# Both scan directions of a bidirectional RWKV-7 mixer in one scheduled list, with bonus sums computed as rows

## The chip, the cores and the metric

The kernel runs on one core of one Trainium2 chip. The metric is the device time of one launch in microseconds (us), measured on the chip; lower is better.

## The reference

One layer of a hybrid backbone is applied to 4096 latent tokens and to 256 context tokens. Each token row of 1024 is normalised, modulated and projected. The projection feeds two branches: (A) a bidirectional RWKV-7 scan with 8 heads of 64, and (B) a chunked gating unit. Both are gated, concatenated and mapped by one output projection; a norm, a gate and the residual follow. Everything is float32. What matters here is the scan of branch A, once forward and once backward over the tokens, with separate parameters per direction:

```python
def step(s, inp):
    r_t, k_t, v_t, w_t, kk_t, b_t = inp
    sa = jnp.einsum('bhvk,bhk->bhv', s, -kk_t)
    s = (s * w_t[:, :, None, :] + sa[..., None] * b_t[:, :, None, :]
         + v_t[..., None] * k_t[:, :, None, :])
    return s, jnp.einsum('bhvk,bhk->bhv', s, r_t)
...
for d in range(2):
    ...
    y_d, s_d = _delta_scan(r, k_d, v, decay, kk, kk * a, s0[d], reverse=(d == 1))
    y = y + y_d
    bonus = bonus + jnp.sum(r * k_d * p['r_k'][d].astype(f32), axis=-1, keepdims=True) * v
```

The latent tokens start from given states, the context tokens from zero; the context's final states are outputs too.

## The kernel before

The program has four stages. phase1a and phase1b norm and project all tokens and leave their results in DRAM: h as a high and a low part (d_h), r and k (d_rk), normalised keys (d_kk), v, the gates and the mixed values of branch B. phase2 is the forward scan, phase3 the backward scan with the output projection. A float32 product of weights is made as three matmuls of high and low parts in the type float32r, so each weight is loaded, cast on ScalarE (ACT) and subtracted on VectorE (DVE) once (split_w, L243 to L245).

A scan handles 34 chunks of 128 tokens, 32 of the latent sequence and 2 of the context, and each chunk holds two halves of 64 tokens. For one chunk the parts are, in the order of the data:

- load_ops: lw, lk, lkn, lr load the inputs (L657 and L661) by DMA; all DMAs of the scans are issued on SyncE's queue (SP).
- prep_ops: tanh and up (L692) give decay and rate; cum (L711) is the running sum of log decay on DVE, once per chunk; z, zr, kg, xa, xk make the scaled keys Z and X; qk and qr make q on GpSimd (POOL). ab0 and ab1 (L769) multiply X with Z into PSUM, and four mask multiplies abm00, abm01, abm11, abm10 (L777) bring them to the tile AB on DVE.
- bon (L794) multiplies q with the block of bonus weights rkb, and bonc (L798) copies the 8 sums per token to the tile bo.
- diag (L786) writes the 16x16 diagonal blocks of AB to DRAM in eight small DMAs, blocks (L821) reads them back, spread over partitions, into Ab. step0 to step14 (L851 and L855, two DVE instructions each) invert them; keepT (L859) and place0, place1 (L864, eight DMAs) put the inverses in place in Qb; flip (L880) transposes them on DVE, and mm0 to mm3 (L873) with wm (L884) and ym0 to ym2 (L893) extend them to 64x64.
- scan_ops: for each half, zs (L933) and av (L941) on TensorE (PE), xsc (L951) on ACT, tu (L957) on PE, uv (L965) on ACT, sm (L970) and ys (L977) on PE, and su (L984, L985) on DVE, which updates the state S. zs of the next half reads S.

The forward scan also carries the projections of branch B (proj: L1042 on PE, h loaded at L1031 in two halves of 1 MB each for every 256 tokens). The backward scan adds the two directions (L1167), normalises (stats, scale, norm), gates, and runs the output projection (part0 to part11, L1260), squares, fin (L1286), finx and keepx. Its single-buffered tiles are zs, mb, the high and low parts of the mixed row (mh, ml), x and the result rows.

The order of the work is written by hand. Tables AT_FWD, AT_PROJ and AT_BWD give each part a time in units; pipeline() adds PERIOD = 30 units for each chunk, sorts all parts of one direction by these times and issues them in that order, so the tables set the order of instructions on each engine and of DMAs on SP. The waits are put in by the framework, from the regions that instructions read and write, and from buffers that come free. Each direction has a list of its own:

```python
evs += [(self.PERIOD * n + at[k], f) for k, f in parts.items()]
with self.tc.manual_schedule():
    for _, f in sorted(evs, key=lambda e: e[0]):
        f()
```

Between the two lists phase2's pools are closed, phase3 opens pools of the same kind, scan_setup builds masks and constants for direction 1, load_gp builds the output gain, gn_w and gn_b are loaded, and eight units of w_out are loaded and split through one staging buffer.

Of the kernel before, what the change touches and what calls it, by code (L numbers as in the profile page):

```python
# [2 lines left out]

# [4 lines left out]
F32 = mybir.dt.float32  # L8
# [17 lines left out]
class Mixer:  # L26
# [10 lines left out]
    def constants(self):  # L37
# [4 lines left out]
        self.stat = self.pool(self.ctx, "stat", bufs=4)  # L42
# [458 lines left out]
    def scan_setup(self, ctx, d):  # L501
        nc, io = self.nc, self.io
        self.d = d
        st = self.pool(ctx, f"st{d}")
        self.kp = self.pool(ctx, f"kp{d}", bufs=1)
        self.s1 = self.pool(ctx, f"s1{d}", bufs=1)
        self.s2 = self.pool(ctx, f"s2{d}", bufs=2)
        self.px = self.pool(ctx, f"px{d}", bufs=1, space=PSUM)
        self.dq = self.pool(ctx, f"dq{d}", bufs=3, space=DRAM)
        self.wup = st.tile([128, 512], F32, name="wup")  # L510
        for i, w in enumerate(("w_up", "a_up")):
            nc.sync.dma_start(self.wup[64 * i : 64 * i + 64], io[w][0, d])

        self.mask = st.tile([128, 2, 2, 64], F32, name="mask")
        sg = 1 if d == 0 else -1
        for X in range(2):
            for sl in range(2):
                for half in range(2):
                    nc.gpsimd.affine_select(
                        self.mask[64 * half : 64 * half + 64, X, sl, :], self.ones[64 * half : 64 * half + 64, 0:64],  # L520
                        pattern=[[sg, 64]], compare_op=ALU.is_ge, fill=0.0,
                        base=-1 if sl == X else 0, channel_multiplier=-sg,
                    )

        self.moff = st.tile([128, 4, 16], F32, name="moff")
        for half in range(2):
            nc.gpsimd.affine_select(
                self.moff[64 * half : 64 * half + 64],
                self.ones[64 * half : 64 * half + 64, 0:1].unsqueeze(2).to_broadcast([64, 4, 16]),
                pattern=[[-16 * sg, 4], [0, 16]], compare_op=ALU.is_ge, fill=0.0,  # L530
                base=-16 if d == 0 else -1, channel_multiplier=sg,
            )
        z = self.zero = 0 if d == 0 else 64
        self.run0 = st.tile([128, 8, 65], F32, name="run0")
        nc.vector.memset(self.run0, 1.0)
        nc.vector.memset(self.run0[:, :, z : z + 1], 0.0)
        self.inc = st.tile([128, 8, 65], F32, name="inc")
        nc.vector.memset(self.inc, 0.0)
        self.lnh = st.tile([128, 1], F32, name="lnh")
        nc.vector.memset(self.lnh, math.log(0.5))  # L540
        self.ka2 = st.tile([128, 4], F32, name="ka2")
        ka = self.ka = self.vT[:, 64 + 4 * d : 68 + 4 * d]
        nc.vector.tensor_scalar(self.ka2, ka, -1.0, 2.0, op0=ALU.mult, op1=ALU.add)
        self.rkb = st.tile([128, 4, 2], F32, name="rkb")
        nc.vector.memset(self.rkb, 0.0)
        rk = self.vT[:, 72 + 4 * d : 76 + 4 * d]
        for hh in range(2):
            sl = slice(64 * hh, 64 * hh + 64)
            nc.vector.tensor_scalar_mul(self.rkb[sl, :, hh], rk[sl], 0.25)
# [14 lines left out]

    @staticmethod
# [11 lines left out]
    def load_state(self, src):  # L577
        nc = self.nc
        if src is None:
            nc.gpsimd.memset(self.S, 0.0)  # L580
            return
        t = self.s1.tile([64, 4, 128], F32, name="stin", tag="q")
        nc.sync.dma_start(t.rearrange("v p (h k) -> v p h k", h=2), src.rearrange("(p h) v k -> v p h k", h=2))
        ps = self.px.tile([128, 256], F32, name="us", tag="us")
        for p in range(4):
            nc.tensor.transpose(ps[:, 64 * p : 64 * p + 64], t[:, p, :], self.ident[:64, :64])
        nc.vector.tensor_copy(self.S.rearrange("p a b -> p (a b)"), ps)

    def store_state(self, dst):
# [765 lines left out]
```

## Time and profile before

| | |
|---|---|
| time, median of 3 runs | 3635.41 us (3626.2 to 3649.29) |
| profiled execution | 3635.12 us, span 3633.4 us |
| TensorE clock granted, mean | 0.947 |
| PE, DVE, ACT, POOL busy | 89%, 57%, 34%, 28% |
| DMA | 429.61 MB, mean 118 GB/s |
| first and last cum forward | 1351.1 and 2383.5 us |
| first and last cum backward | 2477.9 and 3523.2 us |

In the profile L12 is line 12 of the kernel file. A group of instructions is named by line, engine, operation and out<-in, then the count, the busy time in us and the mean in ns of one, then the time for which its engine was idle just before them, with what ended it. PEld is the loading of weights on PE, which overlaps the matmuls. A float32 matmul shows as two instructions. SPq is the DMA queue of SyncE; a DMA's row there is its issue, not its transfer.

### The profile page before, as it was taken

The page shows a single profiled execution, that of the slowest core. Times are in us where ns is not written, and L with a number is a line of the kernel's source. Part 1 is how long each engine was busy: PE and PEld are TensorE (multiplying, and loading weights), DVE is VectorE, ACT ScalarE, POOL GpSimd, SP SyncE. Part 2 cuts the span into 40 slices and gives each one's busy share as a digit, 9 for nine tenths or more (in the row PEclk, how much of TensorE's full clock was granted, in tenths as well). Part 3 has the DMA queues.
Part 4 walks back from the last instruction along what each step waited for, and adds up shares of the span by engine and source line. Part 5 has one row for each costly group of instructions (what it writes and reads, how often), then busy time and mean ns, then how long its engine had stood idle before and what let it go on. Part 6 is the DMA issues. An engine that isn't in the chain of part 4 may idle for free. (4 is left out here: it accounts for less than half of the span.)

```text
span 3633.4 us, 102021 instructions
## 1 busy us (share of the span) xinstructions
PE 3238.2 (89%) x43093; PEld 2692.5 (74%) x43093; DVE 2059.3 (57%) x4969; ACT 1219.5 (34%) x2928; POOL 1005.1 (28%) x1500
## 2 busy tenths in 40 slices
PE   6999998799999968899898889873889899999997
PEld 4777776577887767888888888873777777777776
DVE  4455554322222235666666666654778787787884
ACT  3232231111111123343333333322444444444442
POOL 4444442111111111111111111110344444444443
PEclk9999999899999988999999999985899999999998
DMA  7354344522322133434343433424334444444442
GB/s 261 139 194 154 144 184 168 160 99 93 128 87 99 64 117 95 110 103 118 91 119 99 111 109 104 110 55 104 85 108 120 116 116 119 117 112 113 119 116 69
DMA packets 526870, 429.61 MB, mean 118 GB/s; under 512 B 191051, under 2 KB 458187, under 8 KB 519244
## 3 DMA queue, kind: packets, MB, share of 16 engines
q1 hardware_dynamic: 521386, 413.38, 37.1%
q10 hardware_dynamic: 5026, 9.70, 0.8%
q8 instruction: 339, 5.55, 0.7%
q14 instruction: 119, 0.97, 0.1%
HBM read 275.46 MB, written 147.46 MB: 116 GB/s over the span
## 5 line engine op out<-in xcount | busy, mean ns | idle before, releaser
L1042 PE MATMUL acc<-hld,wAh 128*128 128x256 f32 x2176 | 434.7, 300 | 13.3 <-DMA hld<-d_h 13.3
L1042 PEld LDWEIGHTS acc<-hld,wAh 128*128 128x128 f32 x2176 | 356.6, 201 | 25.1 <-DMA hld<-d_h 16.2
L1042 PE MATMUL acc<-hld,wAl 128*128 128x256 f32 x1088 | 317.6, 292 | 0.0
L851 DVE TENSOR_TENSOR tm<-TP,Ab 128x48 f32<-128x48 f32 (+13 forms) x1020 | 218.1, 214 | 156.1 <-DMA Ab<-dA 126.6
L777 DVE TENSOR_TENSOR AB<-prep,mask 128x512 f32<-128x512 f32 x272 | 177.1, 683 | 125.1 <-PE prep L769 122.0
L855 DVE TENSOR_TENSOR TP<-TP,tm 128x48 f32<-128x48 f32 (+13 forms) x1020 | 225.4, 221 | 35.1
L1260 PE MATMUL acc<-wAh,mh 128*128 128x512 f32 x544 | 242.1, 445 | 3.0 <-DVE on L1286 2.9
L272 PE MATMUL acc<-hl,wAh 128*128 128x512 f32 (+1 forms) x576 | 226.0, 395 | 0.0
L724 POOL TENSOR_TENSOR q<-q,k 128x512 f32<-128x512 f32 x68 | 97.3, 1431 | 457.5 <-ACT q L719 348.2
L1260 PE MATMUL acc<-wAl,mh 128*128 128x512 f32 x544 | 220.2, 405 | 0.0
L1260 PE MATMUL acc<-wAh,ml 128*128 128x512 f32 x544 | 220.1, 405 | 0.0
L272 PE MATMUL acc<-hh,wAl 128*128 128x512 f32 (+1 forms) x576 | 218.6, 384 | 0.0
L1042 PEld LDWEIGHTS acc<-hld,wAl 128*128 128x128 f32 x1088 | 217.8, 200 | 0.0
L272 PE MATMUL acc<-hh,wAh 128*128 128x512 f32 (+1 forms) x576 | 217.7, 393 | 0.0
L769 PE MATMUL prep<-Z,X 64*64 64x128 f32 x4352 | 169.2, 283 | 47.6 <-DVE X L755 42.0
L272 PE MATMUL acc<-hld,wAh 128*128 128x512 f32 (+1 forms) x576 | 175.9, 389 | 16.5 <-ACT wAh L244 11.7
L758 POOL TENSOR_TENSOR q<-q,r 128x512 f32<-128x512 f32 x68 | 99.0, 1455 | 327.5 <-DVE X L755 241.7
L465 PE MATMUL acc<-wAh,hld 128*128 128x512 f32 x544 | 183.6, 402 | 0.0
L769 PEld LDWEIGHTS prep<-Z,X 64*64 64x64 f32 x4352 | 129.7, 137 | 72.5 <-issue 34.8
L253 ACT COPY win<-acc 128x512 f32<-128x512 f32 (+1 forms) x108 | 60.7, 564 | 351.6 <-PE acc L272 334.7
L873 PE MATMUL inv<-Y,W 64*64 64x64 f32 x4352 | 160.8, 224 | 18.4 <-DVE Y L893 17.9
L465 PE MATMUL acc<-wzh,hld 128*128 128x512 f32 x544 | 176.0, 394 | 0.0
(231 smaller groups left out, 7473.9 us busy)
## 6 DMA issues: line engine op xcount, KB each, us to landing
hld<-d_h SPq DMA_DIRECT2D x36, 1024.0 KB
x<-in_x_sample SPq DMA_DIRECT2D x64, 512.0 KB
hld<-d_h SPq DMA_DIRECT2D x16, 2048.0 KB
kn<-d_kk SPq DMA_DIRECT2D x68, 256.0 KB
k<-d_rk SPq DMA_DIRECT2D x68, 256.0 KB
r<-d_rk SPq DMA_DIRECT2D x68, 256.0 KB
UV<-d_v SPq DMA_DIRECT2D x136, 128.0 KB
d_h<-hh SPq DMA_DIRECT2D x16, 1024.0 KB
```

Source lines behind the costliest of these rows:

```text
L253: nc.scalar.copy(w[:, 2 : 2 + n], ps[:, :n])
L272: self.nc.tensor.matmul(ps[:, :n], a[:, k, :], b[:, k, :n], start=(k == 0 and j == 0), stop=(k == NK - 1 and j == 2),)
L465: nc.tensor.matmul(ps, a[:, k, sub], b[:, k % 2, :], start=(k == 0 and j == 0), stop=(k == NK - 1 and j == 2),)
L724: nc.gpsimd.tensor_mul(fl(P["q"]), fl(P["q"]), fl(P["k"]))
L758: nc.gpsimd.tensor_mul(fl(P["q"]), fl(P["q"]), fl(P["r"]))
L769: nc.tensor.matmul(P["pab", pi][hh][o, 128 * p : 128 * p + 128], w, self.slots(P["Z"], p, pi, hh), start=True, stop=True, tile_position=(6 ...
L777: nc.vector.tensor_mul(P["AB"][:, x, 4 * pi : 4 * pi + 4, :], P["pab", pi][hh].rearrange("p (a b) -> p a b", a=4), m)
L851: nc.vector.tensor_mul(tm[:, :nj, :nt], TP[:, js, s : s + 1].to_broadcast([128, nj, nt]), Ab[:, s : s + 1, tt].to_broadcast([128, nj, nt]),)
L855: nc.vector.tensor_sub(TP[:, js, tt], TP[:, js, tt], tm[:, :nj, :nt])
L873: nc.tensor.matmul(ps[h, 64 * j : 64 * j + 64], l(x, h, j), r[h, j, :], start=True, stop=True, tile_position=(64 * x, 64 * x),)
L1042: nc.tensor.matmul(Q["ps", j][:, b, :], x[:, k, :], y[:, k, :], start=(k == 0 and i == 0), stop=(k == NK - 1 and i == 2),)
L1260: nc.tensor.matmul(P["po"][half], a[:, ki, :], b[:, ki % 2, :], start=(ki == 4 and j == 0), stop=(ki == 3 and j == 2),)
```

## The change

The two directions share one set of pools and one list of parts. scan_setup makes what both use; direction(d) makes the small constants of one direction, for both directions ahead of the list. The mask, the decay's origin and the up weights stay single and are rewritten in the list at the turn, by triangle(1) (eight selects on POOL), origin(1) (three small memsets on POOL) and load_up(1). The backward chunks' times start at turn(), the smallest offset at which certain parts of the first backward chunk follow certain parts of the last forward one:

```diff
+    def turn(self):
+        T = self.PERIOD
+        after = (("su1", "zs0"), ("ys1", "zs0"), ("so0", "zs0"), ("so1", "zs1"), ("cum", "gates00"), ("up", "up"))
+        after += tuple((f"abm{i}", "ab0") for i in ("00", "01", "10", "11"))
+        return T * (self.NT // 128) + 3.0 + max(0.0, *(self.AT_FWD[a] + 0.1 - T - self.AT_BWD[b] for a, b in after))
...
+            evs = self.forward(hp, op, pp, self.direction(0))
+            evs += self.backward(hp, op, pp, self.direction(1))
+            T, N = self.PERIOD, self.NT // 128
+            evs += [
+                (T * (N - 1) + self.AT_FWD["up"] + 0.01, lambda: self.load_up(1)),
+                (self.turn() + self.AT_BWD["gates00"] - 0.01, lambda: self.origin(1)),
+                (self.turn() + self.AT_BWD["ab0"] - 0.01, lambda: self.triangle(1)),
+            ]
+            with self.tc.manual_schedule():
+                for _, f in sorted(evs, key=lambda e: e[0]):
+                    f()
```

The backward scan's rows have no pools of their own. When the last part of the forward projections is through, room() takes the three buffers of the forward h tiles (8 KB per partition each) and one of the gate's as boxes, and the tiles become regions of them: box 0 holds the output gain, gn_w and gn_b; box 1 holds mh and ml; box 2 holds x, zs and the result row; box 3 holds v. Before that, boxes 0 and 2 are the staging buffers of w_out, and its split's subtraction moves from DVE to POOL:

```diff
+        def split(i):
+            st = box[2 * (i % 2)][:, 0:1024].rearrange("p (k n) -> p k n", k=2)
+            hi, lo = (self.wA.tile([128, 2, 512], F32R, name=f"wo{x}", tag="wA") for x in "hl")
+            ws[units[i]] = (hi, lo)
+            nc.scalar.copy(hi, st)
+            nc.gpsimd.tensor_sub(lo, st, hi.bitcast(F32))
+
+        at = T * (N - 2) + max(self.AT_PROJ.values()) + 0.1
+        evs += [(at, room), (at + 0.01, lambda: load_gn(0)), (at + 0.02, lambda: load_gn(1)), (at + 10.0, half_gn)]
+        evs += [(at + 0.03 + 6 * i, lambda i=i: load_w(i)) for i in range(8)]
+        evs += [(at + 7.5 + 6 * i, lambda i=i: split(i)) for i in range(8)]
+        evs += [
+            (at + 54.0, lambda: load_gp(0)),
+            (self.turn() + self.AT_BWD["zs0"] - 12.0, lambda: self.fetch_state(box[2][:, 1536:2048], io["state_bwd"][0, 0])),
+            (self.turn() + self.AT_BWD["zs0"] - 0.02, lambda: self.store_state(box[2][:, 1024:1536], io["new_state_fwd"][0, 0])),
+            (self.turn() + T * N + 3 * T, lambda: self.store_state(box[2][:, 1024:1536], io["new_state_bwd"][0, 0])),
+        ]
```

The bonus sums are made as rows, with rkb (32 columns, two of them used) as the weights on four column strips of PE, copied and transposed:

```diff
         def bon():
-            P["pb"] = pb = psum()
-            pbv = pb[:, 0:8].rearrange("t (h p) -> t p h", h=2)
+            P["pb"] = psum()
             for p in range(4):
-                nc.tensor.matmul(pbv[:, p, :], P["q"][:, p, :], self.rkb[:, p, :], start=True, stop=True)
+                nc.tensor.matmul(
+                    P["pb"][32 * p : 32 * p + 32, 0:128], c.rkb[:, p, :], P["q"][:, p, :], start=True, stop=True,
+                    tile_position=(0, 32 * p),
+                )
+        def bonr():
+            P["br"] = s1.tile([128, 128], F32, name="br", tag="br")
+            nc.scalar.copy(P["br"], P["pb"][:, 0:128])
+        def bont():
+            P["pt8"] = psum()
+            nc.tensor.transpose(P["pt8"][:, 0:128], P["br"], self.ident)
         def bonc():
             P["bo"] = s2.tile([128, 8], F32, name="bo", tag="bo", bufs=3)
-            nc.vector.tensor_copy(P["bo"], P["pb"][:, 0:8])
+            nc.vector.tensor_copy(
+                P["bo"].rearrange("t (h p) -> t p h", h=2),
+                P["pt8"][:, 0:128].rearrange("t (p x) -> t p x", p=4)[:, :, 0:2],
+            )
```

The three tables are new throughout; PERIOD stays 30. The times on which the steps below rest, in units, before and after (two parts stand in this order on an engine where their times, taken modulo 30, do):

| AT_FWD | before | after | AT_BWD | before | after |
|---|---|---|---|---|---|
| lw | -80.29 | -79.78 | cum | -56.31 | -61.36 |
| lkn | -71.47 | -65.87 | abm11 | -43.15 | -47.05 |
| lr | -57.13 | -65.43 | abm10 | -41.31 | -46.82 |
| cum | -59.34 | -57.39 | flip | -11.54 | -14.09 |
| abm11 | -41.03 | -39.35 | bon | -39.92 | -46.59 |
| flip | -8.16 | -7.83 | bonc | -37.38 | -40.45 |
| abm10 | -39.71 | -37.61 | loadm | 14.31 | -12.73 |
| bon | -42.79 | -41.52 | loady | -14.54 | -28.41 |
| bonc | -42.57 | -40.43 | loadx | 46.62 | 45.45 |
| ab1 | -42.35 | -40.00 | diag | -38.31 | -41.59 |
| diag | -37.94 | -37.39 | lk | -67.62 | -60.23 |
| blocks | -33.09 | -31.30 | values | -26.08 | -39.32 |
| step0 | -29.12 | -26.30 | lkn | -58.62 | -69.09 |
| zs0 | -1.76 | 6.52 | blocks | -36.46 | -37.50 |
| ys1 | 23.38 | 32.17 | step0 | -33.23 | -36.82 |
| h1 (AT_PROJ) | -63.31 | -68.04 | zs0 | -7.85 | -12.50 |
| p000 (AT_PROJ) | -56.03 | -60.43 | su0 | 4.62 | 0.00 |
| p112 (AT_PROJ) | -40.59 | -39.13 | loadz | 0.69 | -6.36 |
| p312 (AT_PROJ) | -10.37 | -12.61 | gatez | 26.31 | 21.59 |
| | | | keepx | 69.00 | 65.00 |

Smaller edits: the pool of row statistics has 3 buffers instead of 4, the state's load is issued ahead of its use as a part of the list (fetch_state), and the squares' scratch is bfloat16.

More of the change, by code (lines that the diff above doesn't have):

```diff
@@ L2 @@
 from contextlib import ExitStack
+from types import SimpleNamespace
 import concourse.bass as bass
@@ new lines, in triangle @@
+    def triangle(self, d):
+        sg = 1 if d == 0 else -1
+        for X in range(2):
+            for sl in range(2):
+                for half in range(2):
+                    self.nc.gpsimd.affine_select(
+                        self.mask[64 * half : 64 * half + 64, X, sl, :], self.ones[64 * half : 64 * half + 64, 0:64],
+                        pattern=[[sg, 64]], compare_op=ALU.is_ge, fill=0.0,
+                        base=-1 if sl == X else 0, channel_multiplier=-sg,
+                    )
@@ L826, in prep_ops @@
             "tanh": tanh, "up": up, "inc": inc, "cum": cum, "qk": qk, "expg": expg, "expi": expi, "gc": gc,
-            "z": z, "zr": zr, "kg": kg, "xa": xa, "xk": xk, "qr": qr, "diag": diag, "bon": bon, "bonc": bonc,
+            "z": z, "zr": zr, "kg": kg, "xa": xa, "xk": xk, "qr": qr, "diag": diag, "bon": bon, "bonr": bonr, "bont": bont, "bonc": bonc,
             "tkm": tkm, "blocks": blocks,
@@ L1101, in phase2 @@
[L1101 to L1121 removed]
+            self.scan_setup(ctx)
@@ new lines, in finx, with keep @@
+            def finx(half):
+                sl = slice(512 * half, 512 * half + 512)
+                nc.gpsimd.tensor_add(P["x"][:, sl], P["x"][:, sl], P["o", half])
+            def keep():
+                dst = io["y_sample"][0, t0 : t0 + 128] if t0 < self.TS else io["y_prompt"][0, t0 - self.TS : t0 - self.TS + 128]
+                nc.sync.dma_start(dst, P["x"])
+            return begin, sink, {
+                "loady": loady, "loadf": loadf, "loadv": loadv, "bonus": bonus, "bonusv": bonusv, "bonusb": bonusb,
+                "scale": scale, "weigh": weigh, "addb": addb, "loadz": loadz, "gatez": gatez, "loadm": loadm,
+                "splitm": splitm, "splitn": splitn, "turn": turn, "splith": splith, "splitl": splitl,
+                "scaleo": scaleo, "loadx": loadx, "keepx": keep,
+                **{f"stats{h}": lambda h=h: stats((h, h + 1)) for h in (0, 2, 4, 6)},
+                **{f"norm{h}": lambda h=h: norm((h, h + 1)) for h in (0, 2, 4, 6)},
+                **{f"part{i}": lambda i=i: part(i) for i in range(12)},
+                **{f"{f.__name__}{h}": lambda f=f, h=h: f(h) for f in (squares, fin, finx) for h in range(2)},
+            }
@@ L1316, in run @@
+        order = list(range(self.TS - 128, -1, -128)) + list(range(self.NT - 128, self.TS - 1, -128))
+        evs += self.pipeline(self.turn() / T, order, c, pp, more, self.AT_BWD)
+        return evs
     def run(self, upto=9):
```

605 lines of the change are left out of this document (297 added, 308 removed), and 76 rows, old and new, of tables (AT_BWD, AT_FWD, AT_PROJ).

## The prediction

> **What bounds the kernel now.** I read the page first (span, busy shares, clock in 40 slices), then busy time by stage, then the waits of PE, VectorE (DVE) and the DMA queue, then the order of time on DVE and SP inside one chunk.
>
> ```profile
> span 3633.4 us, 102021 instructions
> PE 3238.2 (89%) x43093; PEld 2692.5 (74%) x43093; DVE 2059.3 (57%) x4969; ACT 1219.5 (34%) x2928; POOL 1005.1 (28%) x1500
> PEclk9999999899999988999999999985899999999998
> ```
>
> The run lasted 3635.1 us around this span; the three runs' median is 3635.4, so the sum below can stand for either. PE looks like the bound at 89%, but the clock dips in slices 31 and 32. By stage (columns: us, PE, PEld, DVE, ACT, POOL busy, granted clock, DMA share, GB/s):
>
> ```profile
> 1440.00:2380.00 940.00, 850.24 (x17032) 794.50 (x17030) 599.98 (x1620) 359.46 (x960) 131.12 (x180) 0.97 0.39 107
> 2455.00:2545.00 90.00, 34.80 (x430) 28.31 (x430) 35.99 (x74) 23.19 (x47) 7.39 (x9) 0.51 0.42 105
> 2600.00:3540.00 940.00, 861.34 (x15757) 698.64 (x15755) 753.61 (x2042) 452.30 (x1203) 431.25 (x665) 0.98 0.42 116
> ```
>
> Forward scan (first row) and backward scan (third) keep PE 90 to 92% busy. Between them lie 90 us in which no engine is busy for half of the time. The running sum (cum, L711) comes once per 128-token chunk, so its first and last starts give the pace: forward, across the turn, backward from its third chunk:
>
> ```profile
> L711 DVE TENSOR_TENSOR_SCAN cum<-run,inc x34: 1233/1235/1242, 1351.1 to 2383.5; 128x520 f32<-128x520 f32 x34
> L711 DVE TENSOR_TENSOR_SCAN cum<-run,inc x4: 1233/1234/1236, 2383.5 to 2552.8; 128x520 f32<-128x520 f32 x4
> L711 DVE TENSOR_TENSOR_SCAN cum<-run,inc x32: 1232/1234/1237, 2552.8 to 3523.2; 128x520 f32<-128x520 f32 x32
> ```
>
> Forward 1032.4/33 = 31.3 us per chunk, backward 970.4/31 = 31.3. The three steps across the turn take 169.3 where 3 x 31.3 = 93.9 would be the pace: the turn costs 75 us.
>
> What makes it 31.3, when PE is busy 850.24/940 x 31.3 = 28.3 (forward) and 28.7 (backward)? The waits, forward then backward (us in total, times, longest):
>
> ```profile
> PE us L957 <- DVE tm L851: 44.6, 23, 3.6
> DVE AB L777 <- PE prep L769: 73.9, 41, 5.2
> DVE tm L851 <- DMA Ab<-dA: 71.0, 27, 4.0
> PE xy L933 <- DVE S L985: 61.8, 29, 4.7
> ```
>
> PE waits for DVE, and DVE waits for the DMA that brings the diagonal blocks back (Ab). Two forward chunks and one backward chunk on DVE show the loop:
>
> ```profile
> 2087.01 1.29 DVE L777 TENSOR_TENSOR AB<-prep,mask 128x512 f32<-128x512 f32 x2 [0.42 <-PE prep L769]
> 2102.98 0.17 DVE L851 TENSOR_TENSOR tm<-TP,Ab 128x15 f32<-128x15 f32 x1 [3.30 <-DMA Ab<-dA]
> 2121.51 1.29 DVE L777 TENSOR_TENSOR AB<-prep,mask 128x512 f32<-128x512 f32 x2
> 2133.89 0.17 DVE L851 TENSOR_TENSOR tm<-TP,Ab 128x15 f32<-128x15 f32 x1 [1.37 <-DMA Ab<-dA]
> ```
>
> ```profile
> 2975.51 0.71 DVE L880 STREAM_TRANSPOSE Tb<-Qb 128x512 f32<-128x512 f32 x1
> 2976.14 0.65 DVE L777 TENSOR_TENSOR AB<-prep,mask 128x512 f32<-128x512 f32 x1
> 2987.42 0.17 DVE L851 TENSOR_TENSOR tm<-TP,Ab 128x15 f32<-128x15 f32 x1 [0.57 <-DMA Ab<-dA]
> ```
>
> The last mask multiply (abm10) ends, eight DMAs write the diagonals (diag), one reads them back (blocks), step0 starts, and DVE in its fixed order reaches the next chunk's abm10. Forward that is 14.7 us of transfer (2088.3 to 2103.0), 19.8 of DVE (to 2122.8), 11.1 of transfer, and 62.6 less these, 17.0, of DVE. Backward: 10.6 and some 20.7. So the pace is this loop, not PE.
>
> **The turn** is the largest part. Now a second setup, eight w_out loads and the first chunk's whole preparation run in a row:
>
> ```profile
> 2470.85 26.81 SPq L243 DMA_DIRECT2D wst<-in_w_out  x7
> 2485.95 2.10 PE L769 MATMUL prep<-Z,X 64*64 64x128 f32 x32 [13.78 <-DVE X L755]
> ```
>
> One staging buffer lets the loads pass one at a time, and PE waits 13.8 us for the first X. Afterwards the backward chunks stand in the same list. turn() gives 34 x 30 + 3 + 14.77 units (ys1 against zs0: 32.17 + 0.1 - 30 + 12.50). So the last forward cum (-57.39) and the first backward one (-61.36) are 30 + 17.77 - 61.36 + 57.39 = 43.8 units apart. At 31.3/30 us per unit that is 45.7, and two more backward steps make 108.3, against 169.3: **-61**. If the light engines hold 1.0 us per unit, 103.8 and -65.5.
>
> What is moved under the last forward chunks: eight half-MB w_out loads with 12 DMAs on SP, 4 more for gnw and gnb, eight ACT casts, eight subtractions that go from DVE to POOL, and eight selects for the mask on POOL.
>
> ```profile
> L519 POOL TENSOR_SCALAR_AFFINE_SELECT mask<-ones x16: 232/235/238, 1319.2 to 2407.4; 64x64 f32<-64x64 f32 x16
> ```
>
> The selects are 8 x 0.235 = 1.9 us, before the first backward abm00, with POOL idle. SP's queue is the price: behind each load stand diag, blocks and place, and the load waits for its box until POOL has split the one two before. The forward loop pays 14.7 - 11.1 = 3.6 us where 1 MB (the second half of h) is issued between diag and blocks; at 3.6 per MB, 4 MB cost 14.4 at most, and 0 if they fall elsewhere in the loop. The loads are spread over 48 units, some 1.6 loops, and only those ahead of blocks count: I take **+5**. Fill and end get 1.4 and 1.1 units longer by the tables (lw to cum, cum to keepx): **+2** (-3 to +6).
>
> **Bonus sums as rows.** Four matmuls with q as weights become four with rkb (128x32) as weights on four column strips, then a copy on ACT (bonr), a transpose (bont) and the copy on DVE.
>
> ```profile
> L794 PE MATMUL prep<-rkb,q 128*128 128x2 f32 x216 | 27.7, 250 | 7.4 <-DVE AB L777 7.4
> L692 PE MATMUL prep<-lw,wup 64*128 64x128 f32 x448 | 32.5, 285 | 0.0
> L769 PE MATMUL prep<-Z,X 64*64 64x128 f32 x1728 | 68.3, 276 | 6.9 <-DVE X L755 6.9
> DVE bo L798 <- PE prep L794: 16.5, 27, 0.6
> ```
>
> ```profile
> L1244 PE MATMUL prep<-ident,yt 128*128 128x128 f32 x120 | 19.7, 287 | 0.0
> ```
>
> Now 27.7/27 = 1.03 us of PE a chunk. For 8 instructions of 128 columns the nearest rows give 32.5/448 = 73 ns (two tiles side by side) and 68.3/1728 = 40 ns (four): 0.58 or 0.32, and 0.16 for the transpose. I take four tiles: PE gains 0.55 (bounds 0.3 and 0.55), 37 us over 68 chunks if PE were the bound. It isn't, so I count 0. On the loop the forward order has bon, bonr, bont, bonc between the two mask pairs, and bont takes a second of the two prep buffers, which ab1 needs. DVE already waits 0.6 there; an ACT copy and one more hop add some 0.3 us: **+0.3 per forward chunk** (0 to 0.6). Backward, bon follows ab1: 0.
>
> The Trainium skill, TensorEngine Tiling (Array Packing), Theoretical Speedup, gives up to four times for 32 columns; by that the eight instructions alone would cost a quarter of 1.03, 0.26. Its PSUM Bottleneck speaks against: the copies out may become the limit. The row in which DVE waits 0.6 us for these sums agrees so far.
>
> **The new order forward.** flip moves between abm11 and abm10: +0.7 on DVE's part of the loop, -0.6 because four of the eight diagonal DMAs then go out under it. lkn and lr (256 KB each) now stand between diag and blocks in every chunk: at 3.6 per MB +1.8, or 0 if they hide under the landing of the diagonals. h's second half moves from behind diag to ahead of it in every second chunk. What lies ahead of diag costs by these rows, backward with mb, yt and x (1 MB) just issued, and in the turn with nothing:
>
> ```profile
> 2973.98 0.42 SPq L1281 DMA_DIRECT2D x<-in_x_sample  x1
> ...
> 2975.62 4.82 SPq L786 DMA_DIRECT2D dA<-AB  x8
> 2980.54 0.38 SPq L661 DMA_DIRECT2D k<-d_rk  x1
> 2982.17 0.53 SPq L821 DMA_DIRECT2D Ab<-dA  x1
> ```
>
> ```profile
> 2497.89 3.65 SPq L786 DMA_DIRECT2D dA<-AB  x8
> ```
>
> That is 1.2 us. So: even chunks +1.8, odd ones -3.6 + 1.2 + 1.8 = -0.6, mean +0.6 (-1.2 to +1.8). The projection's matmuls begin 4.4 units earlier in the first half, so that the 19.8 may fall towards 17.0: at most -1.4 a chunk, I take -0.9. With the bonus +0.1: **0 over 33 chunks**, bounds -1 and +1 us, so -33 to +33. tu0's wait for DVE (44.6 us) stays with Ab.
>
> **The new order backward.** flip leaves DVE's part (-0.7), and the first four DMAs no longer go out under it (+0.6). 768 KB instead of 1 MB stand ahead of diag (-0.3), 512 KB instead of 256 behind it (+0.9). flip no longer stops the mask multiplies when the placing is late: -0.7 at most. su0 comes three steps sooner, so PE's 61.8 us in zs1 shrink, off the loop. Sum **-0.25 a chunk, -8** (-33 to +20). The boxes hold what single buffers held, loads and stores in the same turn, so I count 0; their cover is that the regions of one box are tracked apart.
>
> **Sum:** 3635.1 - 61 + 5 + 2 + 0 - 8 = **3573**.
>
> **Rivals.** *A, the loop gets shorter too* (0.18). Forward DVE waits 71.0/27 = 2.6 us a chunk for Ab; if the new order hides half, 33 x 1.3 = 43, and half as much again backward: 3573 - 59 = 3514. For it: PE's 28.3. Against: 512 KB more before blocks.
>
> *B, the turn is eaten by its load* (0.15): all 14 us of w_out and a forward loop 0.8 longer: 3573 + 9 + 26 = 3608.
>
> *C, slower* (0.08): h ahead of diag, on odd forward chunks. Half a MB of x took 5.09 us on the chain that ended last:
>
> ```profile
> 2597.34 5.09 DMA x<-in_x_sample
> ```
>
> Were transfers served strictly in order, h's 1 MB would take 10.2, of which some 2.4 pass before diag: +7.8, and lkn with lr 5.1 - 2.9 = 2.2 on every chunk. Less the 3.6 paid now, (7.8 + 4.4 - 3.6)/2 = 4.3 a chunk, 142 in all: 3715. It decides from 62/33 = 1.9 us a chunk. Against it: the backward dA row, 1.2 us behind as much.
>
> The Trainium skill, DMA: Bandwidth & Descriptors, Queues, rings and completion order, has each engine take one ring's descriptors in order, which is C's rule; the 4.82 against 3.65 agrees in direction, not in size.
>
> *D, the boxes don't overlap as buffers did* (0.02): if box 2 were tracked whole, x (loadx to keepx 19.6 units) and zs (loadz to gatez 28.0) would take turns, 47.6 units a chunk instead of 30: over 33 chunks some 600 us more, 4170.
>
> **Chances.** Forecast 0.57 (3545 to 3605), A 0.18, B 0.15, C 0.08, D 0.02. 1% is 36 us, about what a measurement of this kernel can tell from no change. Faster by over 1% (under 3599): A, nearly all of the forecast's range and a third of B, 0.77. Within: the rest of both, 0.13. Slower: C and D, 0.10. Range 3510 (A; the turn at -65 with both orders at two thirds of their best) to 3625 (B and both orders halfway to their worst).
>
> **What would show it.** Right: the last forward and first backward cum 43 to 50 us apart; no slice of PEclk under 8 in the turn; cum paces of 30.5 to 32; eight short bonus matmuls and a transpose at some 0.5 us a chunk. Wrong: a pace that moves by over 1 us, or DVE's wait for Ab over 4 us a chunk in odd forward chunks (C); casts of w_out on ACT with long waits in the turn (B).

## The result and the profile after

The changed kernel takes 3690.97 us (median of 4 runs, 3680.65 to 3693.08) against 3636.4 for the kernel before on the same chip: a ratio of 1.0143, 95% interval 1.0105 to 1.018. It is slower by 1.4%, where 3573 was forecast. The profiled execution took 3680.65 us around this span; then come the stages (forward, turn, backward) in the columns of the prediction's table:

```profile
span 3678.9 us, 102194 instructions
PE 3241.4 (88%) x43161; PEld 2633.3 (72%) x43161; DVE 2086.1 (57%) x4945; ACT 1246.2 (34%) x2996; POOL 1049.7 (29%) x1519
PEclk9999998899999988999999999978999999999999
```

```profile
1440.00:2380.00 940.00, 833.88 (x16856) 759.55 (x16856) 595.85 (x1612) 366.98 (x976) 133.49 (x179) 0.97 0.39 106
2400.00:2510.00 110.00, 62.35 (x1445) 54.07 (x1447) 58.65 (x135) 38.80 (x90) 35.23 (x35) 0.72 0.37 92
2600.00:3560.00 960.00, 842.35 (x14861) 650.67 (x14859) 739.38 (x1918) 434.52 (x1159) 423.22 (x629) 0.98 0.38 107
```

The hole is gone (the turn has PE busy for 62.35 of 110 us, the clock falls to 7 in one slice instead of 5), yet backward PE is busy for 88% instead of 92. The clock is no cause of the slower backward scan: 0.98 there, as before. The running sum of every chunk, again forward, across the turn, and backward from its third chunk:

```profile
L740 DVE TENSOR_TENSOR_SCAN cum<-run,inc x34: 1232/1234/1243, 1348.2 to 2386.5; 128x520 f32<-128x520 f32 x34
L740 DVE TENSOR_TENSOR_SCAN cum<-run,inc x4: 1232/1234/1234, 2386.5 to 2520.8; 128x520 f32<-128x520 f32 x4
L740 DVE TENSOR_TENSOR_SCAN cum<-run,inc x32: 1228/1233/2326, 2520.8 to 3571.8; 128x520 f32<-128x520 f32 x32
```

With the rows of before, these starts split the whole difference:

| stretch | before | after | difference | predicted |
|---|---|---|---|---|
| start to first cum, and last cum to end | 1461.3 | 1455.3 | -6.0 | +2 |
| forward, 33 steps | 1032.4 | 1038.3 | +5.9 | 0 |
| turn, three steps | 169.3 | 134.3 | -35.0 | -56 |
| backward, 31 steps | 970.4 | 1051.0 | +80.6 | -8 |

So the turn paid, two thirds of what was expected, and the backward loop lost it all: 33.9 us a chunk where it had 31.3.

The same loop still sets the pace. From the end of abm10 to step0 it takes 12.25 us on average (11.0 before), from step0 to the next abm10 21.7 (20.3 before), over 29 backward chunks. DVE's two longest waits backward name both halves (us in total, times, longest):

```profile
DVE AB L806 <- PE prep L798: 61.5, 27, 3.4
DVE tm L894 <- DMA Ab<-dA: 44.4, 26, 3.0
```

First half: SP's queue for one chunk. Between the diagonal blocks' writes and their read stand the two loads of values and the load of lkn, 1.9 us of issue; before, one load of 0.38 stood there.

```profile
3046.28 4.51 SPq L815 DMA_DIRECT2D dA<-AB  x8
3050.90 1.27 SPq L959 DMA_DIRECT2D UV<-d_v  x2
3052.21 0.59 SPq L689 DMA_DIRECT2D kn<-d_kk  x1
3052.98 0.53 SPq L864 DMA_DIRECT2D Ab<-dA  x1
```

Second half: PE, then DVE, of the next chunk. ab0 (L798) comes at 3074.83, behind ys1 (L1020) and the matmuls of part6 and part10 (L1345), and DVE stands idle for 2.04 us ahead of the mask multiply:

```profile
3071.95 0.65 PE L1020 MATMUL xy<-UV,AB 128*64 128x64 f32 x14 [0.16 <-DVE yt L1252]
3072.53 0.50 PE L1345 MATMUL acc<-woh,box 128*128 128x512 f32 x1
...
3074.51 0.40 PE L1345 MATMUL acc<-woh,box 128*128 128x512 f32 x1
3074.83 1.10 PE L798 MATMUL prep<-Z,X 64*64 64x128 f32 x32
```

```profile
3073.35 0.60 DVE L1275 BATCH_NORM_STATS2 s<-yt 128x6 f32<-128x64 f32 x4
3075.99 1.29 DVE L806 TENSOR_TENSOR AB<-prep,mask 128x512 f32<-128x512 f32 x2 [2.04 <-PE prep L798]
```

In the old table ab0 (-45.92, which is 14.08 in a period of 30) stands directly behind ys1 and sm1, with no part of the output projection between. My prediction read DVE's and SP's order out of the tables, and not PE's.

### The profile page after: what moved, and what is told of

Read it like the earlier page. It is cut to its first block, busy times and chain, and to the rows that moved or that the text cites. A ratio compares the mean times of both kernels' runs of the same rounds, so it can differ in the third digit from the quotient of the medians.

```text
span 3678.9 us, 102194 instructions
## 1 busy us (share of the span) xinstructions
PE 3241.4 (88%) x43161; PEld 2633.3 (72%) x43161; DVE 2086.1 (57%) x4945; ACT 1246.2 (34%) x2996; POOL 1049.7 (29%) x1519
## 4 chain that ended last, share of the span: by engine, by line
PE 47%; DVE 22%; DMA 17%; SPq 8%; issue 4%; POOL 1%; ACT 1%; DVEq 0%; POOLq 0%; ACTq 0%
PE acc L273 18%; PE acc L466 10%; DMA Ab<-dA 9%; DVE tm L894 5%; DVE TP L898 5%; SPq L815 4%; PE prep L798 4%; PE acc L1345 3%; PE acc L1101 2%; DVE AB L806 2%; SPq L907 2%; DMA dA<-AB 2%; PE inv L916 2%; DMA wst<-in_w_in 2%; DVE Z L769 1%
## 5 line engine op out<-in xcount | busy, mean ns | idle before, releaser
L1345 PE MATMUL acc<-woh,box 128*128 128x512 f32 x1088 | 424.0, 432 | 9.4 <-DVE box L1335 6.1
L1101 PE MATMUL acc<-hld,wAh 128*128 128x256 f32 x2176 | 414.8, 291 | 0.0
L1101 PEld LDWEIGHTS acc<-hld,wAh 128*128 128x128 f32 x2176 | 334.8, 190 | 18.5 <-issue 7.5
L1101 PE MATMUL acc<-hld,wAl 128*128 128x256 f32 x1088 | 305.6, 281 | 0.0
L1345 PEld LDWEIGHTS acc<-woh,box 128*128 128x128 f32 x1088 | 208.6, 194 | 82.5 <-DVE box L1335 17.5
L1345 PE MATMUL acc<-wol,box 128*128 128x512 f32 x544 | 219.8, 404 | 0.0
L798 PE MATMUL prep<-Z,X 64*64 64x128 f32 x4352 | 189.2, 292 | 33.1 <-DVE X L784 26.9
L787 POOL TENSOR_TENSOR q<-q,r 128x512 f32<-128x512 f32 x68 | 86.9, 1277 | 401.3 <-PE xy L1020 235.8
L1000 PE MATMUL us<-xs,Tt 64*64 64x64 f32 x2176 | 99.6, 232 | 108.6 <-DVE Tt L936 89.8
L798 PEld LDWEIGHTS prep<-Z,X 64*64 64x64 f32 x4352 | 141.0, 142 | 75.9 <-DVE AB L806 26.5
```

Of the source, the lines that this page charges most:

```text
L798: nc.tensor.matmul(P["pab", pi][hh][o, 128 * p : 128 * p + 128], w, self.slots(P["Z"], p, pi, hh), start=True, stop=True, tile_position=(6 ...
L1000: nc.tensor.matmul(P["pu", pi][h, half(p)], P["Tt"][h, 4 * pi + p, :], P["xs", pi][h, half(p)], start=True, stop=True, tile_position=(h.st ...
L1101: nc.tensor.matmul(Q["ps", j][:, b, :], x[:, k, :], y[:, k, :], start=(k == 0 and i == 0), stop=(k == NK - 1 and i == 2),)
L1345: nc.tensor.matmul(P["po"][half], a[:, ki, :], b[:, ki % 2, :], start=(ki == 4 and j == 0), stop=(ki == 3 and j == 2),)
```

## The experiments

The theory after the result: the backward table is at fault, at two places, PE's order (theory 1) and SP's order (theory 2). The rival: boxes that share storage, the shared pools or the bonus rows (theory 3).

A pace or a turn is read from one profiled execution of each kernel. The eleven profiles with the change's forward table differ by 0.4 us a chunk forward, and the ten of the merged list with rows and the old backward table by 0.5 backward (30.6 to 31.1), so a smaller difference between two profiles shows nothing by itself. Each ratio is to the kernel before, measured again beside the run (3620 to 3627 us for the experiments, 3636 for the change), so runs are compared by their ratios.

### The backward table, two places and whole

*e1: ab0 first*, the table's only edit:

```diff
-"ab0": -50.00, ... "ab1": -48.41,
+"ab0": -51.62, ... "ab1": -50.40,
```

> Only PE's order in the backward chunks: ab0 ahead of ys1, ab1 between part6 and part10, as it was before the change. Theory 1 (PE order: ab0 stands behind ys1, which waits for DVE, and behind part6 and part10, so that DVE waits 2.3 us a chunk for the first mask multiply): the part of the loop from step0 to the next abm10 falls from 21.7 to 20.4 us, the backward pace from 33.9 to 32.6, the time by some 40 us to 3650. Theory 2 (SP order: values and lkn are issued between diag and blocks and put the blocks 1.2 us later): nothing of its 1.2 us moves; if it alone is the cause, the time stays at 3690. Theory 3 (boxes or the bonus rows): stays at 3690.

Measured: 3699.53, ratio 1.0209 (1.0188 to 1.0229); pace 34.1. The edit does what it should to its own wait, and the time doesn't follow:

```profile
DVE yt L1252 <- PE xy L1020: 68.7, 26, 3.1
DVE S L1027 <- PE us L1013: 53.7, 27, 2.1
...
DVE AB L806 <- PE prep L798: 5.2, 26, 0.3
```

ab0 now waits for DVE's X, ys1 waits behind it, and DVE, which has so1 ahead of the mask multiplies, waits 2.6 us a chunk for ys1. The wait was moved: from step0 to the next abm10 it takes 22.4 us, where 20.4 was expected. Theory 1 in this form fell.

*e2: blocks first*:

```diff
-"lkn": -69.09, ... "values": -39.32,
+"lkn": -67.30, ... "values": -37.40,
```

> Only SP's order in the backward chunks: values and lkn are issued behind blocks instead of ahead of it. Theory 2: from the end of abm10 to step0 12.25 becomes 11.0 us, the pace 33.9 becomes 32.7, the time falls by some 40 us to 3650. Rival (the transfers that surround the blocks set when they land, not the place in the issue order): the two transfers meet the blocks all the same, 12.0 us or more, time within 10 us of 3690. Theory 1 alone: 3690.

Measured: 3664.96, ratio 1.0119 (1.0081 to 1.0157); pace (3551.7 - 2526.7)/31 = 33.06, that is 0.85 less, and DVE's wait for Ab is halved:

```profile
DVE AB L806 <- PE prep L798: 61.1, 27, 3.4
...
DVE tm L894 <- DMA Ab<-dA: 23.2, 21, 2.6
```

From the end of abm10 to step0 it now takes 11.4 us instead of 12.25, and the other half stays (21.8). Theory 2 holds, for 0.85 of the 1.2 us, by the pace and its own half of the loop; the time alone doesn't tell (the intervals of 1.0119 and of the change's 1.0143 overlap).

*e3: both edits*:

> Both edits together. If theories 1 and 2 are two separate terms of one loop, their gains add: pace 31.4, 3612. If PE or another order becomes the bound between, some 3640. If boxes or bonus rows hold the pace, 3690.

Measured: 3693.17, ratio 1.019 (1.0169 to 1.0211), pace 34.06. With ab0 ahead of ys1 nothing adds up.

*e4: the old table whole*, bonr and bont put between bon and bonc:

> The change with the backward table of before (the two new bonus parts put between bon and bonc). Theories 1 and 2: the whole loss lies in the table, the backward pace comes back to 31.3 to 31.6 and the time to 3600 to 3615, with the turn still some 35 us shorter than before the change. Theory 3 (boxes that share storage, the bonus rows, the shared pools): the pace stays at 33 or more and the time at 3660 to 3690.

Measured: 3594.26, ratio 0.9902 (0.9874 to 0.9931).

```profile
L740 DVE TENSOR_TENSOR_SCAN cum<-run,inc x34: 1233/1234/1242, 1349.5 to 2387.9; 128x520 f32<-128x520 f32 x34
L740 DVE TENSOR_TENSOR_SCAN cum<-run,inc x4: 1233/1234/1234, 2387.9 to 2520.0; 128x520 f32<-128x520 f32 x4
L740 DVE TENSOR_TENSOR_SCAN cum<-run,inc x32: 1232/1234/1237, 2520.0 to 3468.2; 128x520 f32<-128x520 f32 x32
```

Backward is (3468.2 - 2520.0)/31 = 30.6: the table costs 3.3 us a chunk, 102 in all, and boxes, shared pools and rows cost nothing there. The profiled execution (3575.87) is the fastest of the four, 18 us under their median; by the other profiles with this table and rows the cost is 2.8 to 3.2. Theory 3 fell as the cause of the loss; the pace is even 0.7 under that of the kernel before, which asks for a cause of its own (below).

*e5: ab0 directly behind ys1*, with blocks first:

```diff
-"ab0": -50.00, ... "ab1": -48.41,
+"ab0": -51.57, ... "ab1": -50.40,
```

> The new backward table with blocks ahead of values and lkn, and ab0 directly behind ys1 on PE (not ahead of it), ab1 between part6 and part10: in the order of before. The run with ab0 ahead of ys1 only moved the wait, from the mask multiply to DVE's addition that needs ys1 (69 us in 27 chunks). If PE's order of ab0 behind part6 and part10 is the rest of the loss, DVE's wait of 2.26 us ahead of the mask multiply falls to 0.3, the pace from 33.06 to 31.1, the time to 3603. If it isn't, the pace stays over 32.6 and the time over 3650.

Measured: 3607.25, ratio 0.9961 (0.9943 to 0.998); pace (3506.1 - 2533.5)/31 = 31.4. In a period of 30, ab0 is at 8.38 in e3 and at 8.43 here, with ys1 at 8.41: one place ahead of it or one behind is all that differs, and the paces are 34.06 and 31.38. Against e2, getting ab0 from behind the two parts (and ab1 from behind the second) was worth 33.06 - 31.38 = 1.7, all of it in the half that theory 1 names: from step0 to the next abm10 19.9 us instead of 21.8. In e3 the granted TensorE clock falls to half for a while in 23 of 29 such halves, in e5 in one; the halves without a fall take 21.8 and 19.9 us, so 1.9 of the 2.7 us between e3 and e5 are there at full clock.

```profile
DVE S L1027 <- PE us L1013: 59.9, 32, 2.1
...
DVE tm L894 <- DMA Ab<-dA: 1.7, 3, 1.1
DVE AB L806 <- PE prep L798: 1.4, 2, 0.8
```

Both waits that stood at the loop's two halves are gone. 0.8 are left against the old table (e4), 0.6 of it from abm10 to step0 (11.4 us against 10.8), and what ends last ahead of step0 is now DVE's own work: it waits for Ab no more.

*e16: bonusb behind finx0 on GpSimd* (e5 with bonusb 19.95 instead of 19.09), for these 0.8:

> The run with ab0 directly behind ys1, and on GpSimd bonusb behind finx0 instead of ahead of it. Its backward pace was 31.4, with the old backward table 30.6. If DVE's second fin, which waits 0.9 us for finx0, makes part of that 0.8, the pace falls to 31.0 or less, time 3594. If it lies beside the wait for Ab, no change: 31.3 or more.

Measured: 3637.89, ratio 1.0047 (1.0028 to 1.0065); pace (3526.5 - 2527.8)/31 = 32.2, 0.84 worse. fin waits less, but weigh now comes later, and addb waits for it (0.73 a chunk). First the run before this one, then this one:

```profile
L1304 DVE TENSOR_TENSOR yt<-yt,box 128x512 f32<-128x512 f32 x29 | 21.0, 723 | 0.0
```

```profile
L1312 DVE TENSOR_TENSOR yt<-yt,box 128x512 f32<-128x512 f32 x28 | 50.4, 1801 | 1.0
L1304 DVE TENSOR_TENSOR yt<-yt,box 128x512 f32<-128x512 f32 x28 | 19.4, 692 | 20.5 <-POOL yt L1301 20.5
```

A miss that tells something: 0.73 us more on DVE ahead of step0 came out as 0.84 on the pace, so DVE's row of instructions there is the bound of these two kernels. In them gatez (L1312) takes 1.64 to 1.80 us; with the old table it takes 0.69:

```profile
L1312 DVE TENSOR_TENSOR yt<-yt,box 128x512 f32<-128x512 f32 x26 | 18.0, 692 | 0.9
```

That 1.0 us is about as large as what is left; whether it is the cause was not tried.

*e18: the mends together*, e5 with sm1 at 10.00 instead of 14.32, and forward the bonus parts behind abm10:

> The change's own tables with its mends together: forward the bonus parts behind abm10; backward blocks ahead of values and lkn, ab0 directly behind ys1, and sm1 four units earlier, behind part10. If the mends add up, forward falls from 31.6 to 30.9 us a chunk (22 us) as it did with the old backward table. With sm1 as it was, backward was 31.4: DVE waits there 1.85 us a chunk for sm1. If that wait is the 0.8 left against the old table, backward falls to 30.7 and the time is 3560 to 3570; if it lies beside the wait for Ab, backward stays at 31.3 and the time is 3580 to 3590.

Measured: 3609.31, ratio 0.9961 (0.9944 to 0.9977). Forward (2383.0 - 1352.3)/33 = 31.2, 0.6 less than in e5 and 0.4 less than the mean of the eleven profiles with the bonus parts between the masks; backward (3500.0 - 2513.5)/31 = 31.8, 0.4 more, a miss. DVE's wait for sm1 is gone, and wm, the next on DVE, waits 2.55 us for mm0 in its place, since mm0 comes no sooner:

```profile
DVE W L927 <- PE inv L916: 71.5, 28, 2.6
...
DVE S L1027 <- PE us L1013: 0.5, 2, 0.3
```

### The bonus rows and the forward order

*e6: old table, old bonus* (e4 with q as weights and no bonr, bont):

> The change with the backward table of before and the bonus sums as columns again (q as weights, no copy, no transpose). The run with the old table was 0.7 us a backward chunk faster than the kernel before. If the bonus rows bring that (PE's part of the chunk 0.5 us shorter), the backward pace comes back from 30.6 to 31.2 and the time rises by 15 to 20 us, to 3612. If the rows cost nothing and gain nothing, as predicted, backward 30.6 stays, forward falls by up to 0.3 a chunk, and the time is 3585 to 3594.

Measured: 3602.17, ratio 0.9945 (0.9928 to 0.9961, against 0.9902 with rows); backward (3504.5 - 2536.4)/31 = 31.23, where the rows gave 30.59. This profile is 10 us over its median and e4's 18 under, so the two paces differ by more than the times do.

*b1: the kernel before, with the rows alone*:

```diff
-nc.tensor.matmul(pbv[:, p, :], P["q"][:, p, :], self.rkb[:, p, :], start=True, stop=True)
+nc.tensor.matmul(P["pb"][32 * p : 32 * p + 32, 0:128], self.rkb[:, p, :], P["q"][:, p, :], start=True, stop=True,
+    tile_position=(0, 32 * p))
...
-"bon": -42.79, "bonc": -42.57,
+"bon": -39.60, "bonr": -39.30, "bont": -38.90, "bonc": -38.50,
```

> The kernel before with the bonus sums as rows and nothing else (forward the bonus parts stand behind abm10). As predicted (PE is not the bound, rows are worth nothing): paces 31.2 to 31.4 in both directions, time within 8 us of before. If the rows shorten the loop, as columns cost the change 0.64 us a backward chunk: backward pace 30.7, forward 30.7 to 31.0, time 3600, some 25 to 35 us under before.

Measured: 3574.43, ratio 0.9862 (0.984 to 0.9884): 48 us from one small edit.

```profile
L711 DVE TENSOR_TENSOR_SCAN cum<-run,inc x34: 1232/1234/1242, 1353.3 to 2347.2; 128x520 f32<-128x520 f32 x34
L711 DVE TENSOR_TENSOR_SCAN cum<-run,inc x32: 1232/1234/1235, 2515.2 to 3465.7; 128x520 f32<-128x520 f32 x32
```

Forward 993.9/33 = 30.1 (31.3 before), backward 950.5/31 = 30.7 (31.3). The eight matmuls take 0.44 us a chunk and the transpose 0.34, against 1.03 (27.7/27):

```profile
L794 PE MATMUL prep<-q,rkb 128*32 128x128 f32 x544 | 29.9, 293 | 3.5 <-DVE AB L777 3.5
L805 PE MATMUL prep<-ident,br 128*128 128x128 f32 x68 | 22.9, 337 | 58.3 <-ACT br L801 58.3
```

So PE saves a quarter of a microsecond, and the pace falls by 0.65 backward. The saving on the loop is not what does it. By the DVE rows of all 29 steady backward chunks, the half from step0 to the next abm10 takes 19.7 to 20.2 us in 19 chunks of the kernel before and 21.0 to 22.2 in the other ten; in just these ten the granted TensorE clock falls to half for 3.4 us or more. One such half with a fall and one without, in the columns of the prediction's table by stage:

```profile
3051.30:3072.50 21.20, 16.58 (x217) 12.85 (x216) 18.47 (x58) 6.92 (x18) 6.38 (x12) 0.92 0.36 103
3082.50:3102.30 19.80, 18.92 (x271) 14.57 (x270) 18.14 (x59) 9.09 (x24) 6.97 (x12) 1.00 0.44 126
```

With the bonus as columns ten (before) and eleven (e6) of 29 such halves have the fall; with rows one (b1) and one (e4), and one to five in the other nine profiles with this backward table. The halves without it take 19.7 us on average in all four kernels. So the rows don't shorten the backward loop at full clock. The falls become rarer, and ten times 1.7 us in 29 chunks are 0.6 us a chunk, of which b1 keeps 0.05. That is most of the 0.65. In the kernel before the falls mostly follow a late step0: the half ahead of them, abm10 to step0, takes 12.1 us on average, against 10.4 ahead of the others. Why they are rarer with rows no run shows.

Forward the place counts too: before, the sums and their copy stood between the two mask pairs on the loop itself, where DVE waited 0.6 for them. There the steps with full clock fall as well, from 29.9 us to 29.1 in b1, and those with a fall are nine of 29 instead of 15.

*e14: the place alone*, in the new forward table with the old backward one:

```diff
-"bon": -41.52, "bonr": -41.09, "bont": -40.87, "bonc": -40.43,
+"bon": -37.55, "bonr": -37.05, "bont": -36.50, "bonc": -36.00,
```

> The change with the backward table of before, and in the new forward table the four bonus parts behind abm10 instead of between the two pairs of mask multiplies. With old tables the forward pace was 30.3 to 30.8 against 31.5. If the bonus chain between the mask pairs makes that (predicted as +0.3 a chunk), the pace falls to 31.2 or less. If the rest of the new forward order makes it, it stays at 31.4 to 31.9.

Measured: 3569.62, ratio 0.9854 (0.9829 to 0.9879); forward (2368.5 - 1348.7)/33 = 30.9. The eleven profiles with the new forward table as it is have 31.46 to 31.87, so 0.6 to 1.0 a chunk (0.7 in the mean) is the chain of copy, transpose and copy between the mask pairs: predicted as 0.3, with 0.6 as the bound. It is one profile; e18 above, with the same move, has 0.4 less than that mean.

*e11: both old tables* (forward bonus behind abm10; so1 28.4 and keep 28.6, so that the turn's offset is 6.8 units less):

> The change with the tables of before in both directions; forward the bonus parts stand behind abm10, and so1 and keep directly behind ys1 (so that the turn can close up: its offset is 6.8 units less). If the forward order is worth nothing, as predicted, the forward pace is 31.3 to 31.7 and only the turn gains, 7 us: 3587. If the new forward order costs something, the pace falls under 31.2 and the time to 3577 or less; if it gains, the pace is over 31.9 and the time 3600.

Measured: 3541.99, ratio 0.9793 (0.9767 to 0.9819), the fastest here together with the run below and the two reworked turns.

```profile
L738 DVE TENSOR_TENSOR_SCAN cum<-run,inc x34: 1234/1242/1243, 1349.9 to 2364.9; 128x520 f32<-128x520 f32 x34
L738 DVE TENSOR_TENSOR_SCAN cum<-run,inc x4: 1233/1234/1242, 2364.9 to 2488.3; 128x520 f32<-128x520 f32 x4
L738 DVE TENSOR_TENSOR_SCAN cum<-run,inc x32: 1232/1234/1236, 2488.3 to 3449.7; 128x520 f32<-128x520 f32 x32
```

Forward 30.8, backward 31.0, turn 123.4. Expected was a forward pace of 31.3 to 31.7. What makes it lower is the bonus parts' place and, by one profile of e14, 0.1 to 0.6 of the rest of the new forward order (30.9 less the 30.3 to 30.8 of e11, e12, e15 and e17). Of the 78 us that this run gains on the kernel before beside it, the rows alone (b1) give 48; the merged list adds some 30.

### The turn

All of these have the old backward table; without further edit the turn's three steps take 45.0 + 42.5 + 44.6 = 132.1.

*e8: w_out's subtractions on DVE* instead of GpSimd:

> The change with the backward table of before, and w_out's eight subtractions on DVE instead of POOL. Under the subtractions on POOL (2.4 us each) DVE multiplies of 0.68 us took 2.7 to 2.8 in the turn. If that contention makes the turn longer, the intervals of 42.5 and 44.6 lose 4 to 8 us together, the time is 3587. If DVE pays with its own time (eight times 1 to 1.3 us), no change: 3590 to 3600.

Measured: 3590.11, ratio 0.9912 (0.9883 to 0.994); the turn takes 2526.7 - 2397.0 = 129.7 (45.9 + 43.1 + 40.7), and the time can't be told from e4's. Repeated on both old tables (e12):

> As the run before it, and w_out's subtractions on DVE. With the new forward table that took 3.3 us from the turn's second and third interval together: 3584 here. If it was noise, 3587, as the run before.

Measured: 3547.35, ratio 0.9801 (0.9776 to 0.9826), turn 121.3 against 123.4. Some 2 us in the profile both times, nothing in the time.

*e9: one unit of w_out*:

> The change with the backward table of before, loading and splitting only the first of w_out's eight units in the turn (all eight then use it: the output projection is computed with the wrong weights; the matmuls are as many). If w_out's work crowds the turn, its second and third interval (42.5 and 44.6 us) fall together by 15 to 24 us, the time to 3575. If the turn's steps are long for another reason (the scan's own parts of the two directions side by side, the gain), they fall by less than 6 us, and the time is 3588 or more.

Measured: 3582.74, ratio 0.9898 (0.9865 to 0.9931), turn 42.8 + 41.2 + 41.3 = 125.3: by the profile w_out crowds it by 6.8, not by 20, and by 4.6 in the second and third step, which is the branch for another reason. The time doesn't show it (e4 has 0.9902).

*e10: no gain*:

> The change with the backward table of before, without load_gp(0) in the turn: the gain of the latent rows is set to one by GpSimd, nothing else differs. If DVE's six us with PE for the gain, which stand between abm10 and step0 of the second backward chunk, are on the loop, the third interval falls from 44.6 to about 39 us, the time to 3588. If they lie beside the wait for Ab, it stays within 1.5 us.

Measured: 3584.46, ratio 0.9904 (0.9873 to 0.9935), turn 43.3 + 44.1 + 41.5 = 128.9: 3.2 less, as much as the third step lost, and again nothing in the time. e8's third step lost as much (40.7) with the gain in place, and turns of like kernels (e4, e14) differ by 1.4, so the gain's 3 us are an estimate.

*e7: gain and state moved*:

```diff
-(at + 54.0, lambda: load_gp(0)),
+(at + 15.4, lambda: load_gp(0, (0,))),
+(at + 45.4, lambda: load_gp(0, (1,))),
```

> The change with the backward table of before, and in the turn: the output gain is made in two halves under two forward chunks (w_out is staged in the two halves of box 2 alone, so that box 0 is free), the new state's DMA stands behind the next blocks, the state's load 5 units later. If DVE's six us for the gain and the state's DMA ahead of blocks make the third interval of the turn 44.6 us, it falls to 36 and the time by 9 us to 3585. If the w_out split makes it (POOL beside DVE, and the loads), both intervals stay and the time is within 4 us of 3594.

Measured: 3604.21, ratio 0.9944 (0.9925 to 0.9963), turn 140.0, longer by 8. I had placed both halves by forward time; in the list they fell among the backward mask multiplies, on the loop's DVE half:

```profile
2461.81 1.29 DVE L809 TENSOR_TENSOR AB<-prep,mask 128x512 f32<-128x512 f32 x2 [3.19 <-POOL mask L558]
2463.01 0.47 DVE L1196 TENSOR_SCALAR dg<-ident,gl 128x128 f32<-128x128 f32 x2
2464.24 0.71 DVE L1196 TENSOR_SCALAR dg<-ident,gl 128x128 f32<-128x128 f32 x2 [0.76 <-PE prep L1197]
2467.76 0.69 DVE L939 TENSOR_TENSOR Y<-Qb,inv 128x512 f32<-128x512 f32 x1 [2.80 <-PE inv L919]
```

*e15 and e17: the same behind abm10*, on both old tables. In both runs the new state's copy overwrites a part of w_out's seventh unit before it is split, so that the output projection uses partly wrong weights; the instructions are the same.

> The run with the tables of before, and in the turn: the gain in two halves, each directly behind abm10 of the first and of the second backward chunk, where DVE waits for Ab (w_out staged in box 2 alone), the state's DMA behind the next blocks. In the run that left the gain out the turn was 3 us shorter. If this place hides it: the turn's three intervals fall from 123.4 to 119 us, time 3538. If the turn is set by the scan's state passing from one direction to the other, they stay at 122 or more, time 3542.

> The run with the turn reworked, the backward state loaded to box 3 instead of box 2, where a later w_out load overwrote it (that run's scan started backward from wrong values; its time stands). If nothing else changes: turn's three intervals 120 to 122 us, 0.977 of before, about 3540; it would beat the kernel before by 80 us.

Measured: 3546.89, ratio 0.9775 (0.9749 to 0.98), turn 39.2 + 44.5 + 37.8 = 121.5; and 3543.2, ratio 0.9777 (0.975 to 0.9805), turn 41.7 + 43.6 + 36.8 = 122.1. The third step loses 3.4 to 4.4 us, as without the gain, and the second gains 2 to 3: neither is told from e11 by its time. The second step stays at 41 or more in every run with the old backward table, and the third falls under that only in e8, e12, e15 and e17. In the run with one unit of w_out, DVE waits 3.19 us for the mask's selects in the second step, and three waits of over 2 us lie on DVE's half of the loop in the third, where steady backward chunks of e4 wait for 0.4 on average or less:

```profile
2478.41 0.42 DVE L1027 TENSOR_TENSOR S<-S,us 128x256 f32<-128x256 f32 x1 [2.34 <-PE us L1013]
...
2486.76 1.29 DVE L806 TENSOR_TENSOR AB<-prep,mask 128x512 f32<-128x512 f32 x2 [2.09 <-PE prep L798]
2490.14 0.69 DVE L806 TENSOR_TENSOR AB<-prep,mask 128x512 f32<-128x512 f32 x1 [2.09 <-PE prep L798]
```

My reading is that the scan of one chunk and the preparation of the next hand over to each other there, with none of the output's work between to fill the round trips from DVE to PE and back. No run separates it.

## Why the prediction was wrong, point by point

- **The step that failed** is *the new order backward*, put at -0.25 a chunk, -8 (-33 to +20). The stretch came out at +2.6 a chunk, +81, and the order by itself at +3.3 (e4). The step listed DVE's and SP's moves and left out PE's, where ab0 went behind part6 and part10: 1.7 of the 3.3. What stands between diag and blocks was priced by bytes, at 3.6 us per MB; the 512 KB there cost 0.85 (e2), less than the 1.8 of that price. The terms set against it (flip out of DVE's half, and 0.7 "at most" taken in full) don't show: that half takes 19.9 us in e5 and 19.7 with the old table. The last 0.8 are left on DVE, most of it ahead of step0, and their cause stays open. The terms as listed also add up to -0.2, not -0.25.
- **Bonus rows at 0** was wrong in the time: alone they are worth 48 us (b1). PE saves 0.25 us a chunk, below the bounds of 0.3 to 0.55 (the transpose takes 0.34, not 0.16). "It isn't, so I count 0" holds for the backward loop at full clock, which takes 19.7 us on its DVE half with rows and without. No term held the falls of the granted clock, which are rarer with rows. The row of 0.6 us that was put beside the rule on copies out of PSUM shows DVE waiting for PE, so it does not bear on that rule.
- **Forward order 0** came out (+0.2 a chunk), by luck: the rows' gain (-1.16 in a good place) and the loss from the bonus chain between the masks (0.7, predicted 0.3) and from the rest of the order cancel.
- **The turn's -61**: the first step, 45.7 by the tables, is 45.0. The error lies in the two steps behind it, taken at the steady pace: 89.3 instead of 62.6. The crowding by w_out (+5) is about right in size (6.8 by one profile); the gain, priced at nothing, is some 3 by estimate. The mask's selects, counted as hidden because POOL is idle there, were not: with the old backward table, e14 apart, DVE waits for them for 3.0 to 3.8 us (e7's row). In the changed kernel itself they take 4.29 us instead of 1.9 behind a w_out subtraction, but DVE's wait there (1.56) is for PE. One slice of PEclk is at 7, where none under 8 was expected.
- **Boxes 0**: right (e4). **Fill and end +2**: -6.
- **The rivals**: C (slower, through h ahead of diag forward) had the right sign and the wrong place: forward moved by 0.2 a chunk. A's 59 is 64 if it is 43 and half as much again, which changes nothing here. No rival put a loss in the backward order, and +20 was its bound; that is why 3625 was too low an upper end.

The account, with rows and order apart, closes by construction forward, where the order is what is left: -6 at the ends, forward 33 x (-1.16 for rows in a good place, +1.34 for the order with its place of the bonus) = +6, turn -35, backward 31 x (-0.7 for the change with the old table, e4, +3.3 for the new one) = +81.

The version to keep is the merged list with the old tables: 0.979 of the kernel before.

## What to carry to other kernels

When a table reorders work, write out the order of every engine that the loop passes through, PE too, and look at each instruction that the loop waits for: what was put ahead of it, and does that itself wait for the loop? Two neighbouring places can differ by more than the whole gain (ab0 just ahead of ys1 or just behind it: 2.7 us a chunk, 1.9 of it at full clock), and an edit that only moves a wait shows in the waits at once. Where a pace falls by more than an edit saves (0.65 against 0.25 here), set the chunks side by side with the granted clock of each before you put it down to the loop.

## What the runs showed of the hardware

DVE multiplies with both inputs in SBUF stretch while GpSimd works on tensors. In the changed kernel gatez took 1.81 us where it began together with a GpSimd operation on two tensors (1.80 on average), and in e4, with the old table, 0.69; in the turn of the changed kernel a multiply of the same size took 2.80 under a w_out subtraction:

```profile
3054.99 1.27 POOL L1380 TENSOR_TENSOR box<-box 128x512 f32<-128x512 f32 x1
3054.99 1.81 DVE L1312 TENSOR_TENSOR yt<-yt,box 128x512 f32<-128x512 f32 x1
```

```profile
2442.72 2.37 POOL L1224 TENSOR_TENSOR wol<-box,woh 128x1024 fp32r<-128x1024 f32 x1
2442.84 2.80 DVE L769 TENSOR_TENSOR Z<-kn,G 128x512 f32<-128x512 f32 x1
```

In both the DVE row ends some 0.55 us after GpSimd's. The Trainium skill, SBUF — State Buffer, Who interferes with whom, says that a DVE instruction with two SBUF inputs and a GpSimd instruction that reads SBUF lock each other out for the whole of the one that began first; the rows agree but for 0.14 us, since what is left for DVE behind GpSimd is 0.55 and not the whole 0.69 (1.27 + 0.54 = 1.81; 0.12 + 2.80 = 2.37 + 0.55). Work moved from DVE to GpSimd is therefore not off DVE's path where the two meet.

Eight matmuls of 32 columns took 0.44 us in b1, 55 ns each. The Trainium skill, TensorEngine Tiling (Array Packing), Theoretical Speedup, allows up to four times for 32 columns, by estimate 0.26 us from 1.03; here it was 2.3 times.

The granted TensorE clock in these traces is either full or half, and a fall to half lasts 3.4 us or a multiple of it: 0.50 in the kernel before from 3058.6 to 3061.9, inside the first row of the pair shown with b1. A half of the loop with such a fall took 21.4 us on average there, one without it 19.7.
